# A two-layer diffusion backbone on one core: mixer projections in matmuls of 512 columns, and three first-product steps between the modulation quarters at the start

## The chip, the core and the metric

The kernel runs on one core of a Trainium2 chip. The metric is the device time of one execution in microseconds (us). Three runs of the kernel before gave 2222.65 us in the median (2222.18 to 2224.79). The engines have the profile's names: PE is the matrix engine (PEld its weight load), DVE the vector engine, ACT the scalar engine, POOL the general one, SP the one that issues most transfers (DMAs). PSUM is the memory that PE writes, in eight banks of 512 fp32 columns; SBUF is the memory for everything else.

## The reference, cut to what matters

Two layers work on 256 latent and 256 context tokens, 1024 channels wide. Each layer is a gated feed-forward network (FFN), a token mixer and a second FFN. Before each, the tokens are RMS-normed, scaled and shifted by a modulation that is computed from the conditioning vector; behind each comes a gated residual.

```python
x  = x + 0.5*gate * rmsnorm(swiglu(modulate(x), w_in, w_out))   # w_in: 1024 x 5632, w_out: 2816 x 1024
rq, rk, rv, rg, dq, dk, dv, gates = split(h @ w_in)             # the mixer: one projection, 8192 columns wide
y  = (sigmoid(gA) * ret_out + sigmoid(gB) * diff_out) @ w_out
```

The mixer holds two things. Retention (4 heads, rq, rk, rv, and rg as its gate) weighs scores by a decay. Differential attention (8 heads in 4 pairs, dq, dk, dv) takes the difference of two softmax maps. Both are merged by the gates gA and gB. In the last layer the context is needed for keys and values only, and its second FFN is for latent tokens alone.

## The kernel before, in words

Tokens are in four tiles of 128: 0 and 1 latent, 2 and 3 context. Every large product is done in three matmuls on rounded fp32 parts (mm3, L288 to L291): high by high, high by low, low by high. A weight of 128x1024 is loaded (raw, four buffers), cast by ACT into its high part and subtracted by DVE into its low part (split, L113 to L118; tile w, five buffers). The normed and modulated tokens are h, four tiles, made by norm_xn and norm_q (PE transposes at L247, ACT at L251, DVE at L254 and L255).

The FFN's first product goes through 22 steps f, each of 48 matmuls of 512 columns (256 latent and 256 context); the first two steps run in halves of 256 columns, since the latent half of h is ready sooner. Beside it a generator (ada_gen, L128) computes later modulations on DVE, from tiles of a pool of its own, adap.

The mixer cuts its 8192 projection columns into 32 blocks of 256. A block of keys or queries (projT) has the weights stationary and streams 256 tokens; a block of values or gates (proj) has 128 tokens stationary and streams 256 columns of weights. Either way it's 48 matmuls of 256 columns for two token tiles, in one PSUM bank, with two weight tiles to split per block. Attention (diff_attn) and retention (ret_head) are generators: defer() puts one in a queue, each projection ends in tick(), which runs so many of its steps that it ends within a given number of ticks, and need() runs what is left. A step of attention is a score (L594, L595: two maps), its maximum (L596), exponential (L602), scaling and difference (L608, L609), and two steps later a transpose (L621) and the product with the values (L626). The order is that of the block calls at L823 to L845: keys, queries and values of pair 0, then retention's keys and queries, and so on. A scheduler then orders each engine's instructions by program order and readiness; on the chip each engine works strictly in that order.

At the beginning (startup, L878) the first modulation is computed on PE in four quarters of 2 MB of weights each (L908, then L916), and behind each quarter two of the eight k slices of the latent h are made. The context's h follows inside the first FFN. Transfers are issued by SP in program order: small tables, a quarter, two weight halves, a quarter, the context's X, and so on.

Tiles of 4 KB per partition for everything that lives longer (keys, queries, values, outputs) come from a ring of 15 slots (r), PSUM banks from a ring of eight (ps), both in the order in which they came free.

Of the kernel before, what the change touches and what calls it, by code (L numbers as in the profile page):

```python
# [11 lines left out]
F32 = mybir.dt.float32  # L12
# [8 lines left out]
KD = 8  # L21
# [8 lines left out]
LAG = 2  # L30


def build(ctx, tc, a):
# [8 lines left out]
    adap = ctx.enter_context(tc.tile_pool(name="adap", bufs=4))  # L42
# [25 lines left out]
    banks = Ring(psp, "ps", 8)  # L68
    slots = Ring(rp, "r", 15)

    def bank():
        return banks.get([P, 512])
# [21 lines left out]
    nc.sync.dma_start(ccc, a["ccc"])  # L94
    bada = cst.tile([P, L, 9, 8], F32, name="bada")
    nc.sync.dma_start(bada, a["bada"])
    nwc = cst.tile([P, L, 6, 8], F32, name="nwc")
    nc.sync.dma_start(nwc, a["nwc"])
# [6 lines left out]
    def load(src, halves=(0, 1), pl=rawp, nm="raw"):  # L105
        rs = []
        for j in halves:
            r = pl.tile([P, 1024], F32, tag=nm, name=nm)
            nc.sync.dma_start(r, src[:, j * 1024:(j + 1) * 1024])
            rs.append(r)  # L110
        return rs
# [16 lines left out]
    def ada_gen(l, m, out, conds):  # L128
        for u in range(4):
            r = load(a["wada"][l, m * 4 + u], pl=adap, nm="ada")  # L130
            for j in range(2):
                for c in conds:
# [4 lines left out]
                        accum_out=out[:, c, 2 * u + j:2 * u + j + 1])  # L137
            yield
# [157 lines left out]
    def ffn(l, i, st, AB, fetch, pairs, side, nside, after=None, out=None, xctx=None):  # L296
        h, w01 = st
# [3 lines left out]

        def fin_mm(fs, ws, abs_, c0, c1):
            for k in range(KD):
                for f in fs:
                    wt = ws[f][k // 4].rearrange("p s (k n) -> p s k n", k=4)
                    for z in range(2):
                        lw = wt[:, :, k % 4, z * P:(z + 1) * P]
                        mm3(abs_[f][z][:, c0:c1], lw[:, 0], lw[:, 1], h[k // 2][:, k % 2, 0, c0:c1],
                            h[k // 2][:, k % 2, 1, c0:c1], k == 0, k == KD - 1)
# [10 lines left out]
        if len(pairs) == 2:  # L320
            if w01 is None:
                w01 = [fin_w(l, i, 0), fin_w(l, i, 1)]
            ab01 = [[bank(), bank()], [bank(), bank()]]
            fin_mm((0, 1), w01, ab01, 0, 256)
            xs = xctx or norm_xn(CTX, tmp4)
            for q in range(4):
                norm_q(CTX, q, xs, AB, h)
            if xctx:
                slots.put(*xctx)
# [67 lines left out]
    def mixer(l, st, AB, fetch, after):  # L397
# [7 lines left out]
        o, y, M = {}, {}, {}  # L405
# [35 lines left out]
        def proj_w(b):  # L441
            r = load(a["win"][l, b])
            return [split(r[0]), split(r[1])]

        def proj_c(ws, c, ev):
            b0 = bank()
            bk = b0.rearrange("p (j n) -> p j n", j=2)
            for j in range(2):
# [564 lines left out]
```

## Time and profile before

| | us |
|---|---|
| median of three runs | 2222.65 |
| the profiled execution's own time | 2221.16 |
| its span, first to last instruction | 2219.4 |
| PE busy | 2171.0 |
| DVE busy | 1381.9 |
| ACT busy | 863.1 |

The kernel begins with the start (0 to 66 us) and the first FFN; the first layer's mixer takes 408 to 935 us, the last layer's 1662 to 2020 us. A row's idle time is that of the engine just before the instruction, with what ended it. PE's busy time counts an instruction until its result is out, so successive matmuls overlap: the pace is read from the starts, and the mean duration of one isn't the pace.

### The profile page before, as it was taken

The page shows a single profiled execution, that of the slowest core. Times are in us where ns is not written, and L with a number is a line of the kernel's source. Part 1 is how long each engine was busy: PE and PEld are TensorE (multiplying, and loading weights), DVE is VectorE, ACT ScalarE, POOL GpSimd, SP SyncE. Part 2 cuts the span into 40 slices and gives each one's busy share as a digit, 9 for nine tenths or more (in the row PEclk, how much of TensorE's full clock was granted, in tenths as well). Part 3 has the DMA queues.
Part 4 walks back from the last instruction along what each step waited for, and adds up shares of the span by engine and source line. Part 5 has one row for each costly group of instructions (what it writes and reads, how often), then busy time and mean ns, then how long its engine had stood idle before and what let it go on. Part 6 is the DMA issues. An engine that isn't in the chain of part 4 may idle for free. (4 is left out here: it accounts for less than half of the span.)

```text
span 2219.4 us, 32920 instructions
## 1 busy us (share of the span) xinstructions
PE 2171.0 (98%) x13286; PEld 1932.7 (87%) x13286; DVE 1381.9 (62%) x2240; ACT 863.1 (39%) x1379; POOL 127.6 (6%) x245
## 2 busy tenths in 40 slices
PE   7999999999999999999999999999999999998998
PEld 4888888899999999888888888888879999997997
DVE  3899442777767664588234269844348777767554
ACT  3322232645355433432223252223236545445443
POOL 1000000200100010200000020000011010001000
PEclk9999999999999999999999999999999999999999
DMA  8677332122122223266223227853213322345553
GB/s 338 216 253 254 132 121 97 68 70 80 66 77 77 80 85 117 76 209 218 97 102 134 95 92 254 296 184 116 102 57 113 107 84 103 132 152 184 187 184 133
DMA packets 85417, 307.33 MB, mean 138 GB/s; under 512 B 10208, under 2 KB 10416, under 8 KB 85264
## 3 DMA queue, kind: packets, MB, share of 16 engines
q1 hardware_dynamic: 82224, 295.87, 38.1%
q0 software_dynamic: 2752, 8.31, 1.3%
q8 instruction: 104, 1.70, 0.3%
q10 hardware_dynamic: 288, 1.05, 0.1%
q14 instruction: 49, 0.40, 0.1%
HBM read 304.10 MB, written 1.09 MB: 138 GB/s over the span
## 5 line engine op out<-in xcount | busy, mean ns | idle before, releaser
L117 DVE TENSOR_TENSOR w<-raw,w 128x1024 fp32r<-128x1024 f32 x408 | 497.7, 1222 | 462.6 <-ACT w L116 461.5
L289 PE MATMUL ps<-h,w 128*128 128x256 f32 (+1 forms) x2176 | 716.9, 331 | 3.7 <-DVE h L254 2.9
L291 PE MATMUL ps<-h,w 128*128 128x256 f32 (+1 forms) x2176 | 717.3, 330 | 0.4 <-DVE w L117 0.4
L290 PE MATMUL ps<-h,w 128*128 128x256 f32 (+1 forms) x2176 | 717.5, 330 | 0.0
L116 ACT CAST w<-raw 128x1024 fp32r<-128x1024 f32 x408 | 427.5, 1052 | 684.7 <-PE ps L291 613.3
L289 PEld LDWEIGHTS ps<-h,w 128*128 128x128 f32 x2176 | 412.1, 190 | 43.2 <-DVE h L254 4.0
L291 PEld LDWEIGHTS ps<-h,w 128*128 128x128 f32 x2176 | 412.8, 190 | 41.0 <-issue 2.5
L290 PEld LDWEIGHTS ps<-h,w 128*128 128x128 f32 x2176 | 413.3, 190 | 40.1 <-DVE w L117 0.8
L289 PE MATMUL ps<-w,h 128*128 128x256 f32 x1088 | 308.8, 284 | 0.0
L290 PE MATMUL ps<-w,h 128*128 128x256 f32 x1088 | 308.1, 283 | 0.0
L291 PE MATMUL ps<-w,h 128*128 128x256 f32 x1088 | 307.8, 283 | 0.0
L134 DVE CUSTOM_DVE_ANT_0 jd<-ada,r 128x1024 bf16<-128x1024 f32 x224 | 273.6, 1221 | 15.4 <-DMA ada<-wada_dram 10.4
L289 PEld LDWEIGHTS ps<-w,h 128*128 128x128 f32 x1088 | 208.7, 192 | 0.4
L290 PEld LDWEIGHTS ps<-w,h 128*128 128x128 f32 x1088 | 208.7, 192 | 0.3
L291 PEld LDWEIGHTS ps<-w,h 128*128 128x128 f32 x1088 | 208.6, 192 | 0.0
L289 PE MATMUL ps<-w,gs 128*128 128x512 f32 x504 | 196.2, 389 | 0.0
L290 PE MATMUL ps<-w,gs 128*128 128x512 f32 x504 | 196.1, 389 | 0.0
L291 PE MATMUL ps<-w,gs 128*128 128x512 f32 x504 | 196.1, 389 | 0.0
L315 ACT ACTIVATE t<-ps 128x512 f32<-128x512 f32 (+1 forms) x88 | 47.9, 544 | 253.2 <-PE ps L291 249.8
L316 DVE TENSOR_TENSOR r<-ps,t 128x512 f32<-128x512 f32 (+1 forms) x88 | 54.7, 622 | 95.3 <-PE ps L291 69.6
L289 PEld LDWEIGHTS ps<-w,gs 128*128 128x128 f32 x504 | 94.6, 188 | 19.8
L290 PEld LDWEIGHTS ps<-w,gs 128*128 128x128 f32 x504 | 94.6, 188 | 19.6
(169 smaller groups left out, 2164.6 us busy)
## 6 DMA issues: line engine op xcount, KB each, us to landing
raw<-fin_dram SPq DMA_DIRECT2D x176, 512.0 KB, 4.2
ada<-wada_dram SPq DMA_DIRECT2D x128, 512.0 KB, 4.8
raw<-win_dram SPq DMA_DIRECT2D x128, 512.0 KB, 3.5
raw<-fout_dram SPq DMA_DIRECT2D x88, 512.0 KB, 3.5
r<-wada_dram SPq DMA_DIRECT2D x16, 512.0 KB, 10.2
raw<-wout_dram SPq DMA_DIRECT2D x16, 512.0 KB, 3.6
r<-scr POOLq DMA_DIRECT2D x10, 512.0 KB, 4.7
r<-cc_dram SPq DMA_DIRECT2D x7, 512.0 KB, 5.1
```

The source lines that it names most:

```text
L116: keep(nc.scalar.copy(w[:, 0, :], src))
L117: keep(dve.tensor_tensor(out=w[:, 1, :], in0=src, in1=w[:, 0, :], op=ALU.subtract))
L134: dve.tensor_tensor_reduce(out=junk, in0=r[j], in1=cs[c], scale=1.0, scalar=0.0, op0=ALU.mult, op1=ALU.add, accum_out=out[:, c, 2 * u + j: ...
L289: mm(o, lhsT=wH, rhs=xH, start=start, stop=False)
L290: mm(o, lhsT=wH, rhs=xL, start=False, stop=False)
L291: mm(o, lhsT=wL, rhs=xH, start=False, stop=stop)
L315: act(sg[:, :N], ab[0][:, :N], AF.Silu)
L316: dve.tensor_tensor(out=g[f // 2][:, f % 2, :N], in0=ab[1][:, :N], in1=sg[:, :N], op=ALU.mult)
```

## The change

Six parts. (1) The mixer's value and gate blocks are done as ten blocks of 512 columns (wide, tok): one token tile and 24 matmuls of 512 columns per bank, four weight tiles per block. Key and query blocks with both kinds of tokens (projT) stream 512 tokens at once into two neighbouring banks; those for latent tokens alone keep 256. (2) PSUM is one tile, from which a class Banks hands out single banks and pairs; a latent score takes a pair, and one instruction takes the maximum over both maps. (3) The mixer's blocks run in another order, with other numbers of ticks for the deferred generators; retention's decay tables (ret_decay) become the first step of ret_head. (4) In startup three steps of the first FFN's first product run between the modulation quarters, for latent and context tokens together, in 512 columns (fin_part). (5) The first quarter's transfers stand ahead of all others on SP; small tables go over ACT's and POOL's queues. (6) The pool adap is gone: ada_gen takes its tiles from the ring of slots, which has 19.

```diff
+    class Banks:
+        def __init__(self):
+            self.pairs, self.halves, self.of, self.age, self.n = deque(range(4)), [], {}, [0] * 8, 0
...
+        def two(self):
+            p = self.pairs.popleft()
+            b = psum[:, 2 * p:2 * p + 2]
...
+    slots = Ring(rp, "r", 19)
...
+    nc.scalar.dma_start(ccc, a["ccc"])
...
+    wts = [wada0(0)]
+    pool.dma_start(bada, a["bada"])
...
     def ada_gen(l, m, out, conds):
         for u in range(4):
-            r = load(a["wada"][l, m * 4 + u], pl=adap, nm="ada")
+            r = [slot([P, D]) for _ in range(2)]
...
+        def tok(ws, t, ev):
+            bk = bank()
+            for k in range(KD):
+                wt = ws[k // 2].rearrange("p s (k n) -> p s k n", k=2)
+                mm3(bk, h[k // 2][:, k % 2, 0, t * P:(t + 1) * P], h[k // 2][:, k % 2, 1, t * P:(t + 1) * P],
+                    wt[:, 0, k % 2], wt[:, 1, k % 2], k == 0, k == KD - 1)
             flush()
...
+            tick()
...
         def projT(b, pairs, ev):
+            ws = [split(r) for r in load(a["winT"][l, b])]
+            n = 256 * len(pairs)
+            if len(pairs) == 2:
+                b0 = banks.two()
...
+                    mm3(bk[:, j], wt[:, 0, k % 4, js], wt[:, 1, k % 4, js], h[k // 2][:, k % 2, 0, 0:n],
+                        h[k // 2][:, k % 2, 1, 0:n], k == 0, k == KD - 1)
+                if j == 0:
+                    flush()
+                    if len(pairs) == 2:
+                        tick()
+            for c in pairs:
+                ev(c, bk[:, :, c * 256:(c + 1) * 256])
...
                 if c == LAT:
-                    sbk = [bank(), bank()]
+                    b0 = banks.two()
...
-                    dve.reduce_max(mx[:, m:m + 1], sb[m], axis=AX.X)
+                dve.reduce_max(mx, sb, axis=AX.X)
...
-        diff_blocks(0)
-        rkq_blocks(0)
-        need("d0")
-        diff_blocks(1)
-        gB_block(0)
...
+        dv = [slot([P, 2, 512]) for _ in range(2)]
+        ws = wide_w(4)
+        for t in range(2):
+            tok(ws, t, ev_V(dv))
+        norm_pair(CTX, AB, h)
+        for t in range(2, 4):
+            tok(ws, t, ev_V(dv))
+        K.update(mixer_consts())
+        kq = diff_blocks(0)
+        diff_defer(0, kq, dv, pick(5, 4))
+        kq = diff_blocks(1)
+        diff_defer(1, kq, dv, pick(6, 5))
+        need("d0")
+        rkq_blocks(0)
+        rv_block(0, pick(4, 2), pick(8, 5))
+        need("d1")
+        wide(8, QP, ev_gB(0))
...
+            if q:
+                fin_part(h, (2 * q - 2, 2 * q - 1), fs, ws, abs_, 0, 512)
             b2 = bank()
...
-            norm_q(LAT, q, xs[LAT], AB, h)
+            for c in (LAT, CTX):
+                norm_q(c, q, xs[c], AB, h)
+        slots.put(*xs[CTX])
+        fin_part(h, (6, 7), fs, ws, abs_, 0, 512)
```

How the change moves instructions is shown at three places, as they stand in the built programs. The first is PE at the beginning. Before, behind the second quarter (L916 is its last small product, r_199 to r_205 its weights), the latent part of h feeds the first product's first step at once:

```order
L916 MATMUL ps_244<-sel,t_242 128x2 x4
L247 MATMUL ps_345<-ident,t_153 128x128
L247 MATMUL ps_345<-ident,t_165 128x128
L247 MATMUL ps_345<-ident,t_153 128x128
L247 MATMUL ps_345<-ident,t_165 128x128
L289 MATMUL ps_369<-h,w 128x256
L290 MATMUL ps_369<-h,w 128x256
L291 MATMUL ps_369<-h,w 128x256
```

Now, with L975 the modulation's matmuls, L298 the transposes (r_182 and r_194 are the context's normed tiles) and L340 to L342 the three matmuls of a product, PE has:

```order
L975 MATMUL ps<-r_236,cz 32x512
L298 MATMUL ps<-ident,r_194 128x128
L298 MATMUL ps<-ident,r_182 128x128
L298 MATMUL ps<-ident,r_194 128x128
L975 MATMUL ps<-r_238,cz 32x512
L340 MATMUL ps<-h,w 128x512 x4
L341 MATMUL ps<-h,w 128x512
L342 MATMUL ps<-h,w 128x512
L975 MATMUL ps<-r_240,cz 32x512
```

The first product begins in the middle of the second quarter, but behind the context's transposes, which it now needs too.

The second place is PE in the first layer's mixer, during the attention of the first pair of heads. Before (L594 and L595 scores, L621 transposes, L626 products with the values) it ran beside retention's keys and queries:

```order
L594 MATMUL ps_3707<-r_3046,r_3050 128x512
L595 MATMUL ps_3707<-r_3048,r_3050 128x512
L594 MATMUL ps_3708<-r_3047,r_3051 128x512
L595 MATMUL ps_3708<-r_3049,r_3051 128x512
L621 MATMUL ps_3696<-ident,t_3613 128x128 x4
L594 MATMUL ps_3739<-r_3046,r_3050 128x512
L595 MATMUL ps_3739<-r_3048,r_3050 128x512
L594 MATMUL ps_3740<-r_3047,r_3051 128x512
L595 MATMUL ps_3740<-r_3049,r_3051 128x512
L626 MATMUL ps_3695<-r_3052,t_3701 128x128 x4
L621 MATMUL ps_3728<-ident,t_3634 128x128 x4
L289 MATMUL ps_3770<-h,w 128x256
```

Now it runs beside the keys and queries of the second pair (L651 and L652 scores, L678 transposes, L684 products with the values):

```order
L678 MATMUL ps<-ident,t_3330 128x128 x4
L651 MATMUL ps<-r_3105,r_3191 128x512
L652 MATMUL ps<-r_3107,r_3191 128x512
L684 MATMUL ps<-r_2874,t_3420 128x128 x2
L684 MATMUL ps<-r_2875,t_3420 128x128 x2
L678 MATMUL ps<-ident,t_3358 128x128 x4
L684 MATMUL ps<-r_2874,t_3448 128x128 x2
L684 MATMUL ps<-r_2875,t_3448 128x128 x2
L651 MATMUL ps<-r_3104,r_3190 128x256
L652 MATMUL ps<-r_3106,r_3190 128x256
L651 MATMUL ps<-r_3105,r_3191 128x256
L652 MATMUL ps<-r_3107,r_3191 128x256
```

Two more scores of the same four rows follow before the next matmul of a projection, where before a projection's matmuls stood behind every second step.

The third place is DVE in the same stretch. Before (L488 to L501 evict retention's keys, L596 maxima, L598 to L607 small steps):

```order
L488 TENSOR_TENSOR t_3594<-ps_3545,rtab 128x512
L491 TENSOR_TENSOR t_3595<-ps_3545,rtab 64x512 x2
L596 TENSOR_REDUCE mx<-ps_3602 128x1
L493 TENSOR_TENSOR t_3594<-t_3594,t_3595 128x512
L596 TENSOR_REDUCE mx<-ps_3603 128x1
L596 TENSOR_REDUCE mx<-ps_3623 128x1
L501 SCALAR_TENSOR_TENSOR r_3532<-t_3594,r_3531 128x2x256
L598 TENSOR_SCALAR nb<-mx 128x2
L596 TENSOR_REDUCE mx<-ps_3624 128x1
```

Now (L544 to L569 evict the second pair's keys, L653 is a maximum over both maps, L665 and L666 finish a score, L165 is a weight split):

```order
L665 TENSOR_SCALAR t_3358<-t_3358,rc 128x512
L547 TENSOR_TENSOR t_3393<-ps,dtab 32x512
L666 SCALAR_TENSOR_TENSOR t_3358<-t_3358,r_3364 128x512
L547 TENSOR_TENSOR t_3393<-ps,dtab 32x512
L653 TENSOR_REDUCE mx<-ps 128x2
L549 TENSOR_TENSOR t_3392<-t_3392,t_3393 128x512
L569 TENSOR_TENSOR r_3268<-ps,r_3266 64x2x256
L655 TENSOR_SCALAR nb<-mx 128x2
L165 TENSOR_TENSOR w<-raw,w 128x1024
L569 TENSOR_TENSOR r_3268<-t_3392,r_3266 64x2x256
L569 TENSOR_TENSOR r_3269<-t_3392,r_3267 64x2x256
L569 TENSOR_TENSOR r_3269<-ps,r_3267 64x2x256
```

An eviction of two kinds of tokens (ten instructions) now lies among the steps of four scores.

## Rows read from the trace of the kernel before

**Rows 1.** The page: each engine's busy time, share of the span and instructions; and the span in 40 equal slices, the clock that was granted to PE in tenths of full speed.

```profile
PE 2171.0 (98%) x13286; PEld 1932.7 (87%) x13286; DVE 1381.9 (62%) x2240; ACT 863.1 (39%) x1379; POOL 127.6 (6%) x245
...
PEclk9999999999999999999999999999999999999999
```

**Rows 2.** Engines by stretch: from and to (us), length, busy time and instructions of PE, PEld, DVE, ACT and POOL, PE's granted clock, the share of time that the DMA engines were busy, GB/s. In order: most of the start's transfers; the first layer's stretch of the first pair's attention; the same in the last layer; the end of the last mixer; both mixers.

```profile
10.50:26.50 16.00, 14.55 (x65) 5.37 (x65) 7.34 (x21) 4.56 (x9) 2.30 (x5) 1.00 1.03 410
...
448.40:485.60 37.20, 36.13 (x282) 34.10 (x281) 29.97 (x71) 18.09 (x41) 1.23 (x2) 1.00 0.18 57
1695.50:1721.30 25.80, 25.13 (x193) 23.58 (x192) 22.26 (x60) 15.34 (x31) 0.00 (x0) 1.00 0.31 110
...
2019.30:2026.10 6.80, 3.88 (x17) 3.45 (x18) 3.40 (x5) 2.48 (x7) 2.90 (x4) 0.50 0.28 96
415.00:935.00 520.00, 509.54 (x3967) 490.62 (x3966) 346.03 (x682) 233.27 (x443) 45.69 (x88) 1.00 0.24 81
1669.00:2020.00 351.00, 342.39 (x2684) 330.49 (x2683) 261.84 (x454) 183.06 (x301) 25.14 (x47) 1.00 0.34 118
```

**Rows 3.** PE's matmuls over the whole span by line, names and shape: count, busy time in us and mean ns of one, idle time before them. Each product has three such groups (L289, L290, L291), of which the first is shown. "w,h" streams weights over stationary tokens, "h,w" streams tokens over stationary weights.

```profile
L289 PE MATMUL ps<-h,w 128*128 128x512 f32 x960 | 373.9, 389 | 0.0
...
L289 PE MATMUL ps<-h,w 128*128 128x256 f32 x1216 | 343.3, 285 | 3.7 <-DVE h L254 2.9 <-ACT t L251 0.6 <-DVE adaA L921 0.2
L289 PE MATMUL ps<-w,h 128*128 128x256 f32 x1088 | 308.8, 284 | 0.0
```

**Rows 4.** PE in order of time: start (us), duration, what. First and ninth of a run of matmuls of 256 columns, with nothing between but such matmuls (first layer's mixer); first and 28th of one of 512 that streams tokens; first and 20th of one of 512 that streams weights; and the next that PE did after that. The stretches between hold only such matmuls.

```profile
423.03 0.28 PE L289 MATMUL ps<-w,h 128*128 128x256 f32 x1
...
423.99 0.28 PE L291 MATMUL ps<-w,h 128*128 128x256 f32 x1
...
199.79 0.39 PE L290 MATMUL ps<-h,w 128*128 128x512 f32 x1
...
205.91 0.39 PE L290 MATMUL ps<-h,w 128*128 128x512 f32 x1
...
2009.79 0.39 PE L290 MATMUL ps<-w,r 128*128 128x512 f32 x1
...
2014.10 0.39 PE L291 MATMUL ps<-w,r 128*128 128x512 f32 x1
2020.72 1.09 PE L247 MATMUL ps<-ident,t 128*128 128x128 f32 x4 [6.23 <-DVE t L236]
```

**Rows 5.** PE in order of time at the start: the first modulation matmul, ten of them in a row, the small products and the transposes behind a quarter, an early matmul of the first product that waited for h, the first matmul of step f=2 and that of step f=3 of the first product.

```profile
10.56 4.39 PE L908 MATMUL ps<-r,cz 128*32 128x512 f32 x6 [10.56 <-DMA r<-wada_dram]
...
22.08 1.90 PE L908 MATMUL ps<-r,cz 128*32 128x512 f32 x10 [0.23 <-DMA r<-wada_dram]
24.77 1.05 PE L916 MATMUL ps<-sel,t 128*128 128x2 f32 x8 [0.79 <-DVE t L911]
25.68 0.63 PE L247 MATMUL ps<-ident,t 128*128 128x128 f32 x4
...
28.06 0.39 PE L289 MATMUL ps<-h,w 128*128 128x256 f32 x1 [0.61 <-ACT t L251]
...
66.79 0.40 PE L289 MATMUL ps<-h,w 128*128 128x512 f32 x1
...
77.69 0.39 PE L289 MATMUL ps<-h,w 128*128 128x512 f32 x1
```

**Rows 6.** DVE in the first layer's mixer by line, names and shape: count, busy time in us and mean ns of one, idle time before them.

```profile
L117 DVE TENSOR_TENSOR w<-raw,w 128x1024 fp32r<-128x1024 f32 x72 | 87.6, 1220 | 56.6 <-ACT w L116 56.0
L491 DVE TENSOR_TENSOR t<-ps,dtab 32x512 f32<-32x512 f32 x32 | 22.0, 687 | 0.5
L596 DVE TENSOR_REDUCE mx<-ps 128x1 f32<-128x512 f32 x32 | 21.0, 682 | 10.3 <-PE ps L595 10.3
L596 DVE TENSOR_REDUCE mx<-ps 128x1 f32<-128x256 f32 x32 | 12.7, 416 | 3.1 <-PE ps L595 3.0
...
L513 DVE TENSOR_TENSOR r<-ps,r 64x512 fp32r<-64x512 f32 x16 | 11.0, 689 | 6.5 <-ACT r L511 6.1
...
L501 DVE SCALAR_TENSOR_TENSOR r<-t,r 128x512 fp32r<-128x512 f32 x4 | 2.8, 688 | 1.1 <-ACT r L500 1.1
```

**Rows 7.** DVE in order of time during that attention: start, duration, what.

```profile
465.16 1.28 DVE L596 TENSOR_REDUCE mx<-ps 128x1 f32<-128x512 f32 x2
466.36 0.16 DVE L598 TENSOR_SCALAR nb<-mx 128x2 f32<-128x2 f32 x1
...
467.03 1.22 DVE L117 TENSOR_TENSOR w<-raw,w 128x1024 fp32r<-128x1024 f32 x1
468.18 0.17 DVE L605 RECIPROCAL rc<-se 128x2 f32<-128x2 f32 x1
```

**Rows 8.** What PE waited for, longest first: us in total, times, longest. Three rows of the first layer's mixer, then two of the last layer's.

```profile
PE ps L621 <- DVE t L609: 2.7, 4, 0.9
PE ps L247 <- DVE t L236: 2.6, 3, 1.3
...
PE ps L289 <- DVE h L254: 1.8, 1, 1.8
...
PE ps L247 <- DVE t L236: 8.6, 3, 6.2
...
PE ps L289 <- DVE h L254: 0.6, 1, 0.6
```

More of the change, by code (lines that the diff above doesn't have):

```diff
@@ L30 @@
 LAG = 2
+TB = list(range(0, 4)) + list(range(12, 20))
+WB = list(range(4, 12)) + list(range(20, 32))
 def build(ctx, tc, a):
@@ L319, in ffn @@
         f0 = 0
[L320 to L322 removed]
+        if begun is not None:
+            f0 = len(begun)
+            for f in range(f0):
+                fin_ev(f, begun[f])
+        elif len(pairs) == 2:
+            w01 = [fin_w(l, i, 0), fin_w(l, i, 1)]
             ab01 = [[bank(), bank()], [bank(), bank()]]
             fin_mm((0, 1), w01, ab01, 0, 256)
[L325 removed]
+            xs = norm_xn(CTX, tmp4)
             for q in range(4):
                 norm_q(CTX, q, xs, AB, h)
[L328 to L329 removed]
             fin_mm((0, 1), w01, ab01, 256, 512)
@@ L737, in ev_gB, with rg_y, ev_rg, ev @@
             return ev
-        def ev_rg(hd):
-            def ev(c, b):
-                th = tmp2([P, 2, 256])
+        def rg_y(z, t, th):
+            for hl in range(2):
+                ys = y[z, t // 2][:, t % 2, hl * 256:(hl + 1) * 256]
+                dve.scalar_tensor_tensor(out=ys, in0=ys, scalar=gr[:, t, 2 * z + hl:2 * z + hl + 1],
+                                         in1=th[:, hl * 256:(hl + 1) * 256], op0=ALU.mult, op1=ALU.mult)
+        def ev_rg(z, hold):
+            def ev(t, b):
+                if hold:
+                    if t % 2 == 0:
+                        rgs[t // 2] = slot([P, 2, 512])
+                    th = rgs[t // 2][:, t % 2]
+                else:
+                    th = tmp2()
@@ L769, in post @@
-                    banks.put(t0)
-                return post
-            return ev
-        def diff_blocks(u):
+                    tb = bank()
+                    for k in range(4):
+                        nc.tensor.transpose(tb[:, k * P:(k + 1) * P], th[:, k * P:(k + 1) * P], ident)
+                    M[z, t] = slot([P, 2, 512], F32R)
+                    nc.scalar.copy(M[z, t][:, 0], tb)
+                    dve.tensor_tensor(out=M[z, t][:, 1], in0=tb, in1=M[z, t][:, 0], op=ALU.subtract)
@@ new lines, in pick @@
+        def pick(both, lat):
+            return lat if last else both
+        dv = [slot([P, 2, 512]) for _ in range(2)]
[11 more added lines that the diff above has]
+        need("d0")
@@ L843, in mixer @@
-        gB_block(3)
-        merge_blocks(2)
-        merge_blocks(3)
+        dv = [slot([P, 2, 512]) for _ in range(2)]
+        wide(5, BOTH, ev_V(dv))
+        flush()
+        diff_defer(2, kq, dv, pick(6, 4))
+        wide(2, QP, ev_rg(0, False))
+        kq = diff_blocks(3, "d2")
+        diff_defer(3, kq, dv, pick(7, 5))
+        wide(6, QP, ev_gA(0))
+        rkq_blocks(1)
+        need("d3")
+        rv_block(1, pick(4, 2), pick(7, 4))
+        wide(9, QP, ev_gB(1))
+        wide(3, QP, ev_rg(1, True))
@@ L846, in mixer @@
+        need("r3")
+        for c in QP:
+            for j in range(2):
+                rg_y(1, 2 * c + j, rgs[c][:, j])
+            slots.put(rgs[c])
+        wide(7, QP, ev_gA(1))
         flush()
```

308 lines of the change are left out of this document (147 added, 161 removed).

## The prediction

> **What bounds the kernel now.** I read the page first: PE is busy 98% of the span and the clock granted to it reads full in every slice, while DVE is at 62% [rows 1]. So the end is set by how many matmuls there are and how far apart they start, plus PE's waits. Next I looked at stretches: in the first layer's mixer PE is busy 509.5 of 520 us and DVE 346, in the last layer's 342 and 262 of 351 [rows 2]. Even there PE leads, though DVE has far less room than over the whole span. Busy time hides the pace, since successive matmuls overlap, so I took it from starts in the order of time [rows 4]. Eight steps of 256 columns take 423.99 - 423.03 = 0.96 us, 0.120 each; 27 steps of 512 take 6.12, 0.2267 each; the 512s that stream weights instead of tokens take 4.31 for 19, the same 0.227. The matmul is thus not twice as long at twice the columns: two of 256 cost 0.240, one of 512 costs 0.2267, and each join saves 13.3 ns. Last, the list of PE's waits says what isn't pace [rows 8]: transposes of attention behind DVE's L609 (2.7 us in the first mixer), norms (L247, 6.2 at the end of the last mixer), and the context's h at each mixer's start (1.8 and 0.6).
>
> The Trainium skill (TensorE: Matmul & The Clock Gate, "Wait — 56ns, not 53.3ns?") gives a warm matmul its columns at 2.4 GHz and about 2.5 ns more, whatever the size. By that a join would save 2.5 ns; the rows here say 13.3, over five times that, and I go by the rows.
>
> **Part 1, matmuls of 512 in the mixer.** How many pairs are joined? Values and gates ("w,h", 256 columns) are 1088 in each of three groups, 3264 matmuls [rows 3], all in wide blocks now: 1632 pairs. Of "h,w" with 256 columns there are 1216 x 3 = 3648. The first steps of three FFNs in halves are 3 x 192 = 576, the last FFN for latent tokens alone 22 x 48 = 1056; the other 2016 are keys and queries. Six blocks of queries in the last layer stay at 256 (6 x 48 = 288), so 1728 become 864 pairs. Together 2496 pairs x 13.3 ns = **33.2 us**. The 256s whose starts I took are "w,h"; the mean duration of "h,w" is the same but for 1 ns (285 against 284), so I take their pace as equal.
>
> **Part 4 and 5, the start.** Before, step f=3 of the first product begins at 77.69 [rows 5]. Now f=0 to 2 are begun in the quarters, for all 512 tokens. Transfers bound the first 25 us: 410 GB/s [rows 2], that is 1.28 us for 512 KB. The first modulation matmul at 10.56 had the third big tile; the context's last tile is now the eleventh, so at most 10.56 + 8 x 1.28 = 20.8, about 2 earlier if the small tables, now on other queues, don't delay it. Behind it come norm and transposes: 4 to 6.2 us (6.2 is the longest such wait) [rows 4]. So the first product starts at 23 to 27, I take 25. After that PE has 144 matmuls of 0.227 = 32.7; some 24 modulation matmuls at 0.19 (1.90 for ten) = 4.6; three times the small products and two sets of transposes, 1.05 + 2 x 0.63 = 2.3, so 6.9; and in three quarters a wait like today's 0.79 and 0.61, so 4 to 5 with an eviction of DVE between. Sum 25 + 49 = 74, against 77.7: **3.4 us** gained (ends 6, with a first product at 23 and waits of 4, and -1, with 27 and 3 more of waiting, since a product now needs both kinds of h). The 96 pairs joined there are inside this sum. The later quarters don't set it: the last of the 26 big tiles is in by 10.56 + 23 x 1.28 = 40, when PE still has half its products to do.
>
> **Part 3, the context's norm at the mixer's start.** Two tokens of values (2 x 24 x 0.227 = 10.9 us) now stand between the latent norm and the need for the context's h, where one block of 48 x 0.120 = 5.8 stood; the two waits of 1.8 and 0.6 [rows 8] go: **2.4 us**.
>
> **Parts 2 and 3, the attention of the first pair.** Here I see the price. Before, these steps ran beside retention's keys and queries, now beside those of the second pair, whose evictions cost DVE more. For both kinds of tokens, retention's needs six DVE instructions, the other ten (four rotations of L491 for two, four differences of L513 for two of L501), all 0.69 us [rows 6]: 4 x 0.69 = 2.75 more per block, 5.5 for keys and queries. The joined maximum gives a little back: going from 256 to 512 columns adds 682 - 416 = 266 ns, so 150 ns are fixed, and six scores save 0.9. In the first layer's stretch of 37.2 us DVE goes from 30.0 to 34.6 us [rows 2], while PE goes from 36.1 to 34.8 (96 pairs less): 81% of the stretch becomes all of it. In the last layer, queries for latent tokens alone add 3 x 0.69 in place of 2.75: DVE goes from 22.3 to about 26.2, PE from 25.1 to 24.5, so DVE is longer by some 2 us. Before, a full projection's matmuls stood behind every second step; now four scores, two transposes and their products follow each other on PE, and each depends on a small DVE instruction that may stand behind a weight split, as the split from 467.03 to 468.18 held a reciprocal [rows 7]. Ends: no stall but the 2 us by which DVE is longer; or each of the 10 steps in the first layer and 6 in the last waits for one split of 1.22, 19.5, plus 2. At 81% the present wait was 2.7 for four steps, 0.7 each. I take two thirds of the way, **14 us**, because a full DVE leaves no step without a queue and because a score now takes a pair of banks, of which there are four, held until its second exponential.
>
> **At nothing.** Later pairs of attention run in the same mixture of blocks as today, at 67 and 75% of DVE over a mixer [rows 2]. Decay tables move inside DVE's slack. The modulation's tiles share 19 slots, four more than 15 in place of four of their own; if a slot is late, only DVE's junk products are late, due hundreds of us afterwards. The end of the last mixer (6.2 of norm, then 6.8 us in which the granted clock reads 0.50, half of 2.4 GHz [rows 2]) is untouched. A wide block's four weight tiles in five buffers are the last cost at nothing: covered while the previous token's matmuls (5.45 us) run, in which four splits of 1.22 fit; the rival below prices it.
>
> **Sum.** 2221.2 (the profiled execution) - 33.2 - 3.4 - 2.4 + 14 = 2196. The median of the runs is 1.5 above that execution, so **2198 us**. What a measurement here can tell from no change is 0.2%, 4.4 us.
>
> **The rivals.**
>
> PE stays ahead (chance 0.2). The attention's stalls stay at the 0 to 2 us of the lower end, as DVE slips its evictions into free places. For: PE waits only 2.7 us on L621 in a whole mixer with DVE at 81% in that stretch. Against: 34.6 of DVE for 34.8 of PE. Time: 2222.7 - 39 + 1 = 2185, or 2182 if the start gives its 6.
>
> DVE sets the mixer's pace (0.12). Not only the first pair, but all places where both kinds of keys are evicted beside attention, wait for splits. For: DVE at 75% over the last mixer already, and PE 16 us shorter there. Against: those stretches lose no cover by the order. Two more pairs at 0.7 to 1.2 per step add 14 to the 14: 2212. If a wait nears 6 us, the row with clock 0.50 shows what follows it, another 3.
>
> Slower: wide blocks wait for weights (0.05). Where one wide block follows another, four of five buffers are still in use, each comes free only as the last token's matmuls pass it, and the four splits come one after another: up to 4 x 1.22 = 4.9 us per boundary if none were ahead. At some ten such boundaries that is 49, more than the 39 gained; it decides from 3.9 us per boundary. Time 2222.7 - 39 + 49 = 2233. For: L117 is already DVE's largest group, with 56 us idle before it for ACT's cast. Against: matmuls leave a buffer free every 1.36 us, slower than a split.
>
> No saving per matmul (0.05). Streaming weights in fp32 parts at 512 columns could be paced by something else than in rows 4, so that only start and norms remain against the stalls: 2222.7 - 5.8 + (0 to 14), about 2222. Against: the row that streams 512 of weights at 0.227. The Trainium skill's 2.5 ns per matmul would come out here too: 2592 x 2.5 = 6.5 us. Rows 4 do not bear it out.
>
> **How the numbers follow.** The forecast itself has 0.58, its own range 2188 to 2206 from the ends of the stall (2 to 21.5) and of the start. The range that holds 8 in 10 takes in the first rival, below, and the second, above: 2180 to 2214. Faster by over 0.2% means below 2218: the forecast, the first two rivals, a little of the last: 0.9, less 0.02 for what I have not seen. Slower: 0.05 and 0.02 of the last.
>
> **What would show it.** Matmuls of 512 columns (L340 to L342) starting every 0.227 us in the mixers; f=3 at about 74; PE waits on L678, L684 or L651 for DVE, summing to some 14 us, in both layers beside the second pair's keys and queries, with DVE above 90% busy there. Wrong: DVE there with room and no waits (then the first rival), waits at L165's tiles at the start of wide blocks (the third), or a pace other than 0.227.

## The result, and the profile after

The changed kernel takes 2237.74 us in the median of four runs (2237.54 to 2239.08), the kernel before 2223.72 in the runs beside it (2222.18 to 2225.74): a ratio of 1.0065, with an interval of 1.0053 to 1.0078. It is slower by 0.65%, where 1.1% faster was forecast. In the profiled executions the span goes from 2219.4 to 2236.0 us, 16.6 more.

The changed page, against [rows 1]:

```profile
PE 2150.1 (96%) x10694; PEld 1799.5 (80%) x10694; DVE 1377.9 (62%) x2180; ACT 866.1 (39%) x1367; POOL 131.6 (6%) x248
```

PE has 2592 matmuls fewer and is busy for 21 us less, yet its share falls: it waits more. Two stretches of PE in the order of time show that the pace is the one of [rows 4] for both kinds of stream; columns are start, duration, engine, line, what (the two runs of steps counted below hold only such matmuls):

```profile
408.11 0.62 PE L340 MATMUL ps<-w,h 128*128 128x512 f32 x2
...
410.32 0.39 PE L342 MATMUL ps<-w,h 128*128 128x512 f32 x1
...
411.68 0.39 PE L342 MATMUL ps<-w,h 128*128 128x512 f32 x1
...
431.26 0.39 PE L340 MATMUL ps<-h,w 128*128 128x512 f32 x1
...
433.98 0.39 PE L340 MATMUL ps<-h,w 128*128 128x512 f32 x1
```

Six steps from 410.32 to 411.68 and twelve from 431.26 to 433.98 are 0.227 us each. I count each recorded matmul of a mixer at the pace of its shape (0.227 us at 512 columns, 0.120 at 256, some 0.11 at 128), from the last matmul of the FFN ahead of the mixer to the first of the mixer's output product. By that count the first mixer goes from 453.8 to 433.9 us, the last from 321.4 to 308.9: 32.4 us less, where 33.2 were forecast. What remains of each mixer's length is PE's excess over that pace: **17.5 becomes 35.1 us in the first, 8.3 becomes 40.5 in the last**. So 49.8 us of new excess stand against 32.4 saved; the first mixer begins 1.7 us sooner (406.5 against 408.2), and some 0.9 comes behind the last mixer. 49.8 - 32.4 - 1.7 + 0.9 = 16.6, the difference of the spans.

What PE waited for in the first mixer and then in the last (us in total, times, longest), against [rows 8]:

```profile
PE ps L651 <- DVE r L569: 7.3, 3, 5.2
PE ps L651 <- ACT t L659: 6.1, 1, 6.1
PE ps L678 <- DVE t L666: 2.5, 3, 1.0
...
PE ps L340 <- DVE h L305: 0.3, 1, 0.3
...
PE ps L340 <- ACT t L659: 8.7, 3, 6.4
PE ps L678 <- DVE t L666: 6.0, 3, 3.1
PE ps L651 <- DVE r L569: 4.0, 3, 1.5
PE ps L651 <- ACT t L659: 2.0, 1, 2.0
...
PE ps L341 <- DVE w L165: 0.6, 1, 0.6
```

These waits come to 21.0 and 25.3 us, 8.2 and 2.9 before: 35 of the 49.8. The long ones are few. L651 is a score: it waits for the differences of the queries' or keys' eviction (L569), or for an exponential (L659) to release a bank; in the last layer a projection's first matmul (L340) waits for such a bank too. The stretches around them, columns as in [rows 2]: the first pair's attention in the first layer, the wait inside it, what follows that; the same in the last layer.

```profile
453.00:504.00 51.00, 39.85 (x195) 31.88 (x194) 39.44 (x79) 29.41 (x64) 1.28 (x2) 0.93 0.13 42
478.00:484.00 6.00, 1.11 (x10) 0.90 (x8) 3.79 (x7) 5.11 (x9) 0.00 (x0) 0.99 0.29 87
484.00:490.00 6.00, 4.74 (x16) 4.04 (x17) 4.32 (x11) 3.90 (x9) 0.00 (x0) 0.50 0.00 0
1699.40:1743.00 43.60, 31.29 (x150) 24.78 (x149) 30.09 (x50) 26.19 (x48) 0.00 (x0) 0.80 0.19 61
1728.00:1734.00 6.00, 0.00 (x0) 0.00 (x0) 2.50 (x5) 5.87 (x10) 0.00 (x0) 0.64 0.01 3
1734.00:1740.00 6.00, 5.66 (x23) 4.93 (x24) 1.63 (x5) 2.10 (x6) 0.00 (x0) 0.50 0.00 0
```

Over the whole stretch DVE isn't full (39.4 of 51, 30.1 of 43.6). But while PE stands, ACT works almost without a gap (5.1 and 5.9 of 6 us). And behind each of the two long waits PE's granted clock reads 0.50, 1.2 GHz, for another 6 us, in which 4.7 and 5.7 us of PE's time are spent at half the pace: some 5 us more for the two together. [Rows 2] show the same at the end of the last mixer after a wait of 6.2.

Beside the fourth pair it is DVE that is full. The rows show the granted clock of three more stretches, then DVE's 11.45 of 11.5 us in the last layer, then the two waits, of which the second is the one in that stretch:

```profile
716.00:719.40 3.40, 3.01 (x7) 2.46 (x8) 2.88 (x5) 0.07 (x1) 0.00 (x0) 0.50 0.11 43
1716.10:1722.90 6.80, 4.83 (x16) 3.16 (x15) 5.96 (x16) 3.70 (x11) 0.00 (x0) 0.50 0.24 77
1917.40:1924.20 6.80, 6.05 (x20) 5.37 (x21) 5.45 (x12) 3.82 (x10) 0.00 (x0) 0.50 0.58 207
...
1907.00:1918.50 11.50, 5.53 (x25) 3.65 (x24) 11.45 (x21) 6.11 (x16) 0.61 (x1) 0.95 0.55 184
...
716.39 0.80 PE L651 MATMUL ps<-r,r 128*128 128x512 f32 x1 [5.16 <-DVE r L569]
...
1916.74 0.66 PE L678 MATMUL ps<-ident,t 128*128 128x128 f32 x4 [3.12 <-DVE t L666]
```

In all, the clock reads 0.50 for 10.2 us of the first mixer and 23.9 of the last; before, both read 1.00 [rows 2]. These stretches are most of the 14 or 15 us of new excess that aren't waits: their length, less PE's waits in them and less their matmuls at the usual pace, is 12.6 us, an estimate. By place, 32 us of the 49.8 stand beside the first pair (16.4 and 19.2 in the stretches of above, 2.4 and 1.5 before in those of [rows 2]) and 18 beside the fourth (8.8 and 12.1, 2.1 and 0.7 before).

What ACT does at the first long wait, in order of time:

```profile
481.31 0.58 ACT L571 CAST r<-ps 64x512 fp32r<-64x512 f32 x1
481.89 1.87 ACT L572 CAST r<-r 64x512 fp32r<-64x512 f32 x3
483.78 0.58 ACT L567 CAST r<-ps 64x512 fp32r<-64x512 f32 x1
484.38 0.69 ACT L659 ACTIVATE t<-ps,nb 128x512 f32<-128x512 f32 x1
484.39 0.69 DVE L569 TENSOR_TENSOR r<-ps,r 64x512 fp32r<-64x512 f32 x1 [2.54 <-ACT r L567]
...
485.21 0.58 PE L651 MATMUL ps<-r,r 128*128 128x256 f32 x1 [6.10 <-ACT t L659]
```

These are casts of the eviction of K1, the second pair's keys. A key eviction of both kinds has twelve (L567, L571, L572, four each), 0.58 to 0.62 us apiece, 7.2 us; retention's keys have two (L500 before). The exponential stands behind them on ACT, and PE's next score behind the exponential's bank.

### The profile page after: what moved, and what is told of

The parts are those of the page before. It is cut to its first block, busy times and chain, and to the rows that moved or that the text cites. A ratio compares the mean times of both kernels' runs of the same rounds, so it can differ in the third digit from the quotient of the medians.

```text
span 2236.0 us, 27616 instructions
## 1 busy us (share of the span) xinstructions
PE 2150.1 (96%) x10694; PEld 1799.5 (80%) x10694; DVE 1377.9 (62%) x2180; ACT 866.1 (39%) x1367; POOL 131.6 (6%) x248
## 5 line engine op out<-in xcount | busy, mean ns | idle before, releaser
L165 DVE TENSOR_TENSOR w<-raw,w 128x1024 fp32r<-128x1024 f32 x408 | 497.6, 1222 | 442.5 <-ACT w L164 438.6
L340 PE MATMUL ps<-h,w 128*128 128x512 f32 (+1 forms) x1856 | 664.5, 360 | 8.4 <-ACT t L659 7.4
L341 PE MATMUL ps<-h,w 128*128 128x512 f32 (+1 forms) x1856 | 664.2, 358 | 0.0
L342 PE MATMUL ps<-h,w 128*128 128x512 f32 (+1 forms) x1856 | 662.3, 358 | 0.4 <-DVE w L165 0.4
L340 PEld LDWEIGHTS ps<-h,w 128*128 128x128 f32 x1856 | 352.4, 191 | 63.3 <-ACT t L659 8.3
L341 PEld LDWEIGHTS ps<-h,w 128*128 128x128 f32 x1856 | 353.1, 190 | 50.1 <-issue 0.8
L342 PEld LDWEIGHTS ps<-h,w 128*128 128x128 f32 x1856 | 352.2, 190 | 50.3 <-DVE w L165 0.8
L184 DVE CUSTOM_DVE_ANT_0 jd<-r,r 128x1024 bf16<-128x1024 f32 x224 | 273.3, 1220 | 6.4 <-DMA r<-wada_dram 1.6
L340 PE MATMUL ps<-w,h 128*128 128x512 f32 x544 | 212.6, 392 | 3.7 <-ACT t L659 3.1
L341 PE MATMUL ps<-w,h 128*128 128x512 f32 x544 | 212.8, 392 | 0.6 <-DVE w L165 0.6
L342 PE MATMUL ps<-w,h 128*128 128x512 f32 x544 | 212.3, 391 | 0.0
L340 PE MATMUL ps<-w,gs 128*128 128x512 f32 x504 | 196.2, 389 | 0.0
L342 PE MATMUL ps<-w,gs 128*128 128x512 f32 x504 | 196.1, 389 | 0.0
L340 PEld LDWEIGHTS ps<-w,h 128*128 128x128 f32 x544 | 102.2, 188 | 25.1 <-ACT t L659 4.0
L341 PEld LDWEIGHTS ps<-w,h 128*128 128x128 f32 x544 | 102.2, 188 | 21.7 <-DVE w L165 2.2
L342 PEld LDWEIGHTS ps<-w,h 128*128 128x128 f32 x544 | 102.2, 188 | 20.6
L340 PEld LDWEIGHTS ps<-w,gs 128*128 128x128 f32 x504 | 94.6, 188 | 19.8
L342 PEld LDWEIGHTS ps<-w,gs 128*128 128x128 f32 x504 | 94.6, 188 | 19.7
```

The costliest lines, as they stand in the source:

```text
L165: keep(dve.tensor_tensor(out=w[:, 1, :], in0=src, in1=w[:, 0, :], op=ALU.subtract))
L184: dve.tensor_tensor_reduce(out=junk, in0=r[j], in1=cs[c], scale=1.0, scalar=0.0, op0=ALU.mult, op1=ALU.add, accum_out=out[:, c, 2 * u + j: ...
L340: mm(o, lhsT=wH, rhs=xH, start=start, stop=False)
L341: mm(o, lhsT=wH, rhs=xL, start=False, stop=False)
L342: mm(o, lhsT=wL, rhs=xH, start=False, stop=stop)
```

## The experiments

Four theories of what PE stands for were held against each other. A: ACT's casts of a key block that runs beside attention. B: DVE's larger evictions, as predicted, only with more effect. C: PSUM in four pairs, so that too few banks come free. D, from the fifth experiment on: missing cover, that is, too little work of PE between a block and the first step of attention that needs its eviction. Before, a pair's value block (48 matmuls for each kind, 11.5 us) stood between its queries and its first score, and retention's blocks came behind it; now the first score of the first, second and fourth pairs follows 24 matmuls (5.4 us) after the queries, and only the third pair still has a value block there. All times are medians of at least three rounds; "before" was 2222.5 to 2224.6 beside them. "Excess" is that of the first and of the last mixer, counted as above in the profiled execution. A single stretch of 3.4 us at half clock costs up to 1.7 us and came and went between runs, also in places that an edit doesn't touch, so differences of 2 to 5 us have no exact share of a cause.

**Another order for the first pair.**

```diff
-        kq = diff_blocks(1)
-        diff_defer(1, kq, dv, pick(6, 5))
-        need("d0")
         rkq_blocks(0)
+        need("d0")
+        kq = diff_blocks(1)
+        diff_defer(1, kq, dv, pick(6, 5))
```

> The changed kernel with one move: retention's first keys and queries come again before the second pair's, so that the first pair's attention (d0) runs beside them as in the kernel before. Theory A (ACT: the twelve casts of a key eviction, some 0.6 us each, stand ahead of the exponentials, and PE waits for the banks) and theory B (DVE's ten instructions, as predicted, only larger) both expect the stalls beside K1 and Q1 (16 us in the first layer, 19 in the last) to fall to about 2 to 4 each: 2237.7 - 28 = 2210 (2203 to 2217). Theory C (PSUM in four pairs is what stalls, whatever runs beside) expects at least half of it to stay: 2222 or more.

Measured: 2229.26 us, 8.5 less than the changed kernel, a third of what A and B asked for; most of the excess stays, 31.7 and 34.3 us. Beside the first pair it fell (16.4 to 6.2 in the first layer, 19.2 to 9.8 in the last), but not to the 2.4 and 1.5 of before, and the second pair now lost 9.3 and 8.0 beside retention's values. There stands, from 515 to 560 us:

```profile
PE ps L651 <- DVE r L569: 4.5, 1, 4.5
```

That is again a first score that waits for its own queries' eviction. The time lies in the range of C (2222 or more), but C had not said that the wait would move to another pair with the load, nor had A or B; from this came D. C is tried by itself below.

**Six casts on POOL.**

```diff
-                        nc.scalar.copy(H[m][oth, :, sl], q[own])
-                        nc.scalar.copy(Lo[m][oth, :, sl], Lo[m][own, :, sl])
+                        if c == LAT:
+                            pool.tensor_copy(out=H[m][oth, :, sl], in_=q[own])
+                        else:
+                            nc.scalar.copy(H[m][oth, :, sl], q[own])
+                        pool.tensor_copy(out=Lo[m][oth, :, sl], in_=Lo[m][own, :, sl])
```

> The changed kernel with six of the twelve casts of a key eviction (the copies into the other half: both of L572 for each kind, and L571 for latent tokens) on POOL instead of ACT. Theory A: 6 x 0.62 = 3.7 us less of ACT ahead of the exponential in each layer's first stall (6.3 and 6.5 us), and a little at the later pairs: 2237.7 - 8 = 2230 (2224 to 2233). Theory B (DVE): DVE's queue is the same, within 2 us of 2237.7. Theory C: the same, within 2 us.

Measured: 2232.48 us, 5.3 less. In the first layer's stretch the wait for the exponential fell from 6.1 to

```profile
PE ps L654 <- ACT t L662: 2.8, 1, 2.8
```

(L662 is L659 here), by 3.3 of the 3.7 expected. The first mixer's excess fell by 8.9 to 26.2, though it began 2.1 us later (up to 1.7 of them a stretch at half clock at 399.5 us, in the FFN); the last's stayed at 40.2. So A is part of it, not the whole.

**Scores in single banks.**

```diff
-                    b0 = banks.two()
-                    sb = b0
+                    bs = [bank(), bank()]
+                    sb = bs
...
-                dve.reduce_max(mx, sb, axis=AX.X)
+                    dve.reduce_max(mx[:, m:m + 1], sb[m], axis=AX.X)
```

> The changed kernel with a latent score's two maps in two single banks and two maxima of 512 columns, as before, instead of a pair and one maximum over 1024. Theory C: the 18.6 us that PE waits for L659 (banks held by a score) fall by half or more, 2228 or less. Theories A and B: the exponential comes as late as before, so the bank does too; each score costs DVE 0.15 us more: 2237 to 2241.

Measured: 2235.75 us, 2 less. That lies in neither range, nearer to that of A and B than to C's, and decides nothing by itself. The first mixer's excess rose (to 41.2), the last's fell (to 30.3), so the banks move waits about without setting their sum.

**Keys and queries in 256 columns**, each kind into a single bank:

```diff
-            n = 256 * len(pairs)
-            if len(pairs) == 2:
-                b0 = banks.two()
...
+            for c in pairs:
+                b0 = bank()
...
+                flush()
+                ev(c, bk)
+                banks.put(b0)
+                tick()
```

> The changed kernel with keys and queries streamed again per kind of tokens, 256 columns into one bank, evicted kind by kind; the order and the wide blocks stay. If the joined matmuls give what rows 4 say and nothing else moves: 864 x 13.3 ns = 11.5 us more, 2249. Theory A: the eviction comes in two parts of six casts, the first already done when the second kind's matmuls run, which gives some 8 back: 2241 (2236 to 2246). Theory C: four pairs no longer tied up by keys, more than 11 back: 2237 or less.

Measured: 2242.67 us, 4.9 more, in A's range: the matmuls cost 11.3 at their pace, and 8.2 of excess went (30.9 and 36.5).

**The kernel before without its cover.**

```diff
+            wv = proj_w(20 + u)
+            proj_c(wv, LAT, ev_V(dv))
+            if u == 0:
+                norm_pair(CTX, AB, h)
+            proj_c(wv, CTX, ev_V(dv))
...
+            projT(16 + u, BOTH, ek)
+            projT(12 + u, QP, eq)
-            proj(20 + u, BOTH, ev_V(dv))
```

> The kernel before with one move: each pair's value block stands ahead of its keys and queries instead of behind them, so that the first score comes 11.5 us of projection earlier after the queries' last matmul, as in the changed kernel. Everything else (256 columns, single banks, what runs beside the attention) is of before. Theory D (cover: the value block hid the evictions of keys and queries, and now attention's steps queue behind them on DVE and ACT): 2 to 4 us more stall for each of eight pairs: 2222.7 + 24 = 2247 (2235 to 2257). Theory A (only the casts of a key block that runs beside the attention count) and theory C (pairs of banks): no change, 2220 to 2227.

Measured: 2236.5 us, 14 slower than before (ratio 1.0063, 1.0048 to 1.0078). That is just inside D's range and outside that of A and C, with no 512 columns, no pairs of banks and no other change of order. But all of it lies in the last mixer, whose excess went from 8.3 to 23.1; the first's went from 17.5 to 16.4. So in the first layer the lost value block alone cost nothing, and in the last it cost about half of the 32 us that were lost there in the changed kernel. The last layer's queries are for latent tokens alone and cover a key eviction with 5.8 us instead of 11.5; that this is why only it loses was not tried by itself. What PE waited for there, which the kernel before has not:

```profile
PE ps L594 <- DVE r L513: 6.1, 4, 1.9
PE ps L594 <- ACT t L602: 2.2, 3, 1.1
```

The first is four first scores, one for each pair, that wait for their own operands.

**Attention begun later in the changed kernel.** A deferred generator gets a number of ticks in which it isn't run (hold); the first pair may run on beside retention's first keys, and what is left of it runs ahead of retention's queries.

```diff
-            if sideq:
+            if sideq and clock[0] > sideq[0][4]:
...
-        diff_defer(0, kq, dv, pick(5, 4))
+        diff_defer(0, kq, dv, pick(7, 6), 2)
...
-        diff_defer(1, kq, dv, pick(6, 5))
-        need("d0")
-        rkq_blocks(0)
+        diff_defer(1, kq, dv, pick(9, 9), 2)
+        rkq_blocks(0, "d0")
...
-        diff_defer(3, kq, dv, pick(7, 5))
+        diff_defer(3, kq, dv, pick(8, 6), pick(2, 2))
```

> The changed kernel with attention begun later: the first pair's waits two ticks (so K1 stands between its queries and its first score) and may run on beside retention's first keys, the second pair's waits two ticks, the fourth pair's two. Theory D: the stalls of the first pair (16 and 19 us) and the fourth (8 and 12) fall to the size of the third pair's, which has its value block as cover (4 and 2): 30 to 40 us less, 2203 (2196 to 2212). Theory A: the first pair's steps still stand behind K1's twelve casts, so only the fourth pair gains: 2225 or more.

Measured: 2217.05 us, 20.7 less than the changed kernel and faster than before (0.9977, 0.9967 to 0.9986). D expected 2196 to 2212, A 2225 or more: D's mechanism holds in direction, with some six tenths of its size, and most of it in the last mixer (excess 29.8 and 24.5). The edit also changes over how many ticks the second and fourth pairs' steps are dealt, so it isn't cover alone. The fourth pair's waits went in the last layer; the first pair's didn't all go, since K1's eviction now meets it: in the last mixer

```profile
PE ps L340 <- ACT t L659: 5.8, 2, 4.3
PE ps L651 <- DVE t L547: 4.9, 1, 4.9
```

**The two together**, with the six casts of above on POOL:

> The kernel of the run before this one (attention begun later) with six of a key eviction's twelve casts on POOL. If ACT's casts and the missing cover are two names of one queue, little is left to gain: 0 to 3 us less than without. If they add, 5 less, as they were in the changed kernel (2232.5 against 2237.7).

Measured: 2214.08 us, 3 less (excess 26.0 and 23.5). That is the upper end of what two names of one queue would give (0 to 3) and short of what two separate causes would (5): mostly the same queue.

**Steps given out twice as often** (on top of that): a tick in the middle of each 24 matmuls, twice as many ticks for each generator.

```diff
+                if k == 3:
+                    tick()
...
-            sideq.append([gen, clock[0] + within, steps + 1, key, clock[0] + hold])
+            sideq.append([gen, clock[0] + 2 * within, steps + 1, key, clock[0] + 2 * hold])
```

> The run with attention begun later and six casts on POOL (2214.1), and the deferred steps given out twice as often: also in the middle of every 24 matmuls, half as many steps at a time. If the stalls left (26 us in the first mixer, 24 in the last) come from steps that stand behind each other on PE with no projection between, they fall by a third to a half: 2196 (2190 to 2206). If they come from what DVE and ACT have to do in all, or from too few banks, nothing changes: 2211 to 2217.

Measured: 2204.81 us, 9.3 less; excess 25.1 and 14.4. It was the last mixer that gained. Three steps had come in one tick in both layers, so why the first gained so little this run doesn't show.

**The same alone in the changed kernel**, without holds and with all casts on ACT:

> The changed kernel with the deferred steps given out twice as often, and nothing else (attention begins as early as in the changed kernel, all casts on ACT). If bunched steps alone are what PE stands for: the 9 us that this gave with attention begun later, or more, 2228 or less. If the steps stand behind the evictions of K1 and Q1 in ACT's and DVE's queues however they are dealt out (theory D): 0 to 4 us, 2233 to 2238; the first scores then even come sooner, with still less cover.

Measured: 2233.28 us, 4.5 less, half of what the ticks gave with cover; it lies inside D's range of times (2233 to 2238) by 0.3. The excess rose to 45.4 in the first mixer and fell to 26.4 in the last: alone, the ticks helped one layer and hurt the other. The waits changed their names: 12.0 us in the first mixer for the copy behind a transpose, with the longest 7.8, and 7.4 still for the queries' differences:

```profile
PE ps L687 <- ACT t L683: 12.0, 7, 7.8
PE ps L654 <- DVE r L572: 7.4, 3, 5.2
```

**Attention begun later, keys and queries in 256 columns** (both edits above):

> The run with attention begun later (2217.1), with keys and queries of both kinds streamed in 256 columns into single banks. The matmuls alone cost 11.3 us more: 2228. Theory C (a joined block's pair of banks leaves too few for scores) expects more than that back: 2217 or less. Theory D alone: 2225 to 2231.

Measured: 2229.83 us, 12.8 more than with 512. The joined matmuls are worth what [rows 4] say, and their pairs of banks cost nothing that this frees: C falls, as far as keys and queries go.

**Steps dealt out to the end.**

```diff
-        diff_defer(0, kq, dv, pick(7, 6), 2)
+        diff_defer(0, kq, dv, pick(6, 5), pick(2, 1))
```

> The run with steps given out twice as often (2204.8), with the first pair's steps dealt so that none is left over to be run at once behind retention's first keys (there PE stood some 10 us in the first layer, 6 beside the second pair's queries in the last). If that remainder is bunched steps: 5 to 10 less, 2197 (2193 to 2201). If DVE has simply more to do in that stretch than PE (K1, Q1, retention's keys, their splits and ten steps are some 46 us of DVE for 40 of PE): the wait moves and nothing is gained, 2202 to 2207.

Measured: 2200.6 us (0.9898 of before, 0.9882 to 0.9915), 4.2 less: in the range of bunched steps by 0.4, but not all of it is theirs. In the profiled executions the first mixer's excess fell by 6.0 to 19.1, as expected; the last's rose by 4.4 to 18.8. Some 3 us of the gain come from two places outside both stretches, in which the run before this one has the granted clock at 0.50 and this one doesn't:

```profile
399.10:402.50 3.40, 3.40 (x14) 3.27 (x15) 1.39 (x3) 2.47 (x6) 0.00 (x0) 0.50 0.00 0
907.70:911.10 3.40, 3.40 (x14) 3.23 (x15) 1.42 (x3) 2.51 (x6) 0.00 (x0) 0.50 0.00 0
```

Why the clock fell there in the one run and not in the other stays open. The run is the fastest kernel of the study, 37 us ahead of the changed one, with the same matmuls. What is left in its last mixer:

```profile
PE ps L340 <- ACT t L665: 3.5, 1, 3.5
PE ps L341 <- DVE w L165: 3.0, 2, 2.1
```

**The start** (on top of that): the first quarter's eviction ahead of the norms, the context's X ahead of the weights.

```diff
+            if q == 0:
+                xs[LAT] = norm_xn(LAT, tmp4)
+                for t in range(2, 4):
+                    nc.sync.dma_start(X[t], a["xin"][t])
+                xs[CTX] = norm_xn(CTX, slot)
```

(moved behind the quarter's matmuls and copy; the weight halves behind that).

> The run before this one, with the start changed: the first quarter's eviction comes ahead of the norms and splits, and the context's X is loaded ahead of the first weights. In the changed kernel PE waited 5.0 us for that eviction (it stood behind two norms and two splits on DVE), its granted clock read 0.50 from 18 to 28 us, and the first product began at 28.8 instead of the 25 forecast. Expected: the wait falls to 1 to 2 us, the context's X lands some 3.8 us earlier, the first product begins at 25 or 26, and the whole is 3 us shorter than the run before this one (2 to 5).

Measured: 2203.89 us, 3.3 more, where 2 to 5 less were expected. The wait for the eviction fell from 4.2 to 2.0 (L991 below), and the first product began at 27.05 instead of 28.89, but two other waits came in its place, and the clock read 0.50 until 33 us, 2 longer than in the run before:

```profile
PE ps L298 <- DVE adaA L996: 4.2, 1, 4.2
PE ps L340 <- DVE h L305: 2.0, 1, 2.0
PE ps L991 <- DVE t L976: 2.0, 1, 2.0
```

The step behind the three early ones began 2.4 us later than in the run before (79.1 against 76.7). The context's transposes now stand on PE ahead of the second quarter's matmuls; that this is what cost the time was not tried.

## Why the prediction was wrong

**The joined matmuls**: right. 33.2 us forecast, 32.4 counted in the mixers, and 12.8 lost when 864 of the joins were undone with attention begun later, 14.8 ns each. The Trainium skill's 2.5 ns per matmul (TensorE: Matmul & The Clock Gate, "Wait — 56ns, not 53.3ns?") would have made 2.2 us of these 864, an estimate; the run bears out the rows.

**The start**: right in direction, half in size. Forecast 3.4 us, the mixer begins 1.7 earlier. (The forecast's own parts, 25 + 49 = 74, are 3.7 below 77.7, not 3.4.) The first product was put at 23 to 27 us and began at 28.82:

```profile
18.86 1.87 PE L985 MATMUL ps<-sel,t 128*128 128x2 f32 x8 [5.00 <-DVE t L978]
...
28.82 1.67 PE L340 MATMUL ps<-h,w 128*128 128x512 f32 x4
```

The mis-sized term is the chain in front of it: the quarter's eviction stood on DVE behind two norms and two splits, PE idled for 5.0 us, and then, from 18 to 28 us, worked at a granted clock of 0.50:

```profile
18.00:28.00 10.00, 7.07 (x22) 3.47 (x22) 5.14 (x13) 4.33 (x12) 3.52 (x7) 0.50 1.03 413
```

The next step of the first product began at about 76 us, 47 behind the first, where 49 were forecast.

**The context's norm**: right. Of 1.8 and 0.6 us [rows 8], 0.3 is left in each mixer.

**Attention**: this step failed, as "I take two thirds of the way, 14 us", and so did "Later pairs of attention run in the same mixture of blocks as today" among the terms at nothing. The 14 were for the first pair, where 32 were measured; the fourth pair, at nothing, lost 18. Together that is the 49.8, but for rounding: 35 of waits, and most of the rest half clock behind them, which the sum had at nothing too. Four things were wrong.

First, the price of an eviction was counted on DVE alone. The 2.75 us more of DVE per block were counted from the right instructions (ten against six), but the sign "DVE above 90% busy there" did not come beside the first pair: 39.4 of 51 and 30.1 of 43.6 us are 77 and 69%. The twelve casts on ACT were never counted, and they stood in front of the exponentials; taking six of them off gave back 3.3 of a wait of 6.1.

Second, the upper end allowed one split of 1.22 us for each step. It looked at how busy an engine is, not at how long a chain is. An eviction, a maximum, an exponential, a difference and a copy pass to and fro between DVE and ACT in fixed order, and a step behind a whole eviction waits for all of it. Nor was the present wait read rightly: the 2.7 us for four steps are those of the whole first mixer; in the stretch with DVE at 81% there was one wait of 0.9.

Third, "those stretches lose no cover by the order", said against the second rival, was false. Keys, queries and then values became values, then keys and queries, and the value block had been the cover. On the kernel before alone, this reordering costs 14 us, all of it in the last mixer; in the changed kernel, beginning attention later gave 20.7 back, 16.0 of excess in the last mixer and 5.3 in the first. In the first mixer it took the casts, the ticks and the dealing out as well to come from 35.1 to 19.1. The old order of blocks in the changed kernel was not run. I had read the order at the three places where instructions move together, and not asked what had stood between a pair's queries and its first score.

Fourth, the later pairs were put at nothing by the share of DVE over a whole mixer (67 and 75%). Beside the fourth pair, which has lost its value block too, DVE was busy for 11.45 of 11.5 us in the last layer.

Of the rivals, the second (DVE sets the pace, also at other pairs) was nearest in kind: the stalls came at other pairs too, mainly at the fourth. It had 28 us for it, and one engine where there were two. The first, no stalls, is refuted by the waits. The third gave 2233 us, near the measured time, but that is luck: its mechanism was wrong, since weights at L165 cost 0.6 us in the last mixer. The last, no saving per matmul, is refuted by the pace.

How much of the 49.8 is ACT's casts, how much the missing cover and how much the bunched steps is not settled as a sum. Alone, in the changed kernel, six casts give 5.3, the ticks 4.5 and the later beginning 20.7; one after the other they give 20.7, 3.0 and 9.3, and dealing the first pair's steps out another 4.2. They overlap, as parts of one queue. The half clock behind the long waits is in most of these differences.

## What to carry to other kernels

When an order is changed, list for each consumer what stands between it and its producer before and after, in microseconds of the bound engine: work that was only next in line may have been the cover. Price an eviction on every engine that it passes through, and compare a wait with the length of its chain, not with the engines' busy shares. And a saving on the bound engine shrinks the cover of everything that ran beside it.

## What the runs showed that was not expected

A wait of 5 to 6 us of PE costs more than itself: behind those of 6.1, 5.2 and 6.4 us in the mixers the granted clock read 0.50 for 6.8, 3.4 and 10.2 us, and at the wait of 5.0 at the start for nearly 14. Twice it did so after several shorter waits, none over 3.1 us (from 1716 and from 1917 us). And moving casts of 64x512 to POOL paid although POOL is slower at them (0.79 and 1.01 us against 0.62 on ACT), since POOL had little else to do there (1.28 us of the 51 in the changed kernel's first stretch):

```profile
L575 POOL CAST r<-r 64x512 fp32r<-64x512 f32 x16 | 12.2, 786 | 0.5
L572 POOL CAST r<-t 64x512 fp32r<-64x512 f32 x8 | 8.0, 1005 | 53.2 <-DVE t L549 52.9
```
